# A two-layer diffusion trunk on one core: four-tile first pieces, weight and modulation loads a step ahead, single tiles in the whole half-steps

## The chip, the cores and the metric

One program on one core of a Trainium2 chip. The metric is device time in microseconds; three runs of the kernel before are given, and one more execution that the hardware profiler recorded. The engines are TensorE (PE, matmuls; PEld its weight loads), VectorE (DVE), ScalarE (ACT), GpSimd (POOL) and SyncE (SP, which issues most transfers).

## The reference, cut to what matters

512 latent tokens and 256 context tokens of width 1024 go through two layers. All numbers are fp32.

```python
for l in range(2):
    mx = split(silu(c) @ w_mod[l] + b_mod[l], 9)       # latent: shift, scale, gate, three times
    my = split(silu(c_ctx) @ w_mod[l] + b_mod[l], 9)   # context
    x = x + 0.5 * mx[2] * swiglu(modulate(rmsnorm(x), mx[0], mx[1]), w1[l,0], w3[l,0], w2[l,0])
    # y (context) alike with my
    ox, oy = mixer(modulate(rmsnorm(x), mx[3], mx[4]), ...)   # pooling | retention | convolution
    x = x + mx[5] * ox
    x = x + 0.5 * mx[8] * swiglu(modulate(rmsnorm(x), mx[6], mx[7]), w1[l,1], w3[l,1], w2[l,1])
    # y alike, except behind the last layer's mixer input, where it is no longer needed
return rmsnorm(x) * final_g
# swiglu(h) = (silu(h @ w1) * (h @ w3)) @ w2, with 2816 = 22 x 128 hidden columns
# modulate(h, shift, scale) = h * (1 + scale) + shift
```

## The kernel before

Activations lie with features on the 128 partitions and tokens along the columns; latent is a group of 512 columns, context one of 256. Every product of high precision is three matmuls (`mm3`, lines 162 to 167): operands are split into a high part that ScalarE rounds (line 159) and a low part that VectorE gets by subtraction (line 160), and high x high, high x low and low x high are added in PSUM.

**Weights.** `weight_order` (519) lists all weight blocks in the order of use. `fetch` (566) asks SP for a block into one of five `raw` buffers, `parts` (575) splits it into one of four `wh` and `wl` buffers, and `blocks` (582) does one after the other; `weights` (624) keeps up to four split blocks ahead. An item that is a list (two blocks, `w1` and `w3` of a halved tile) is fetched as soon as the item before it is split; a plain item is fetched only when its own turn to be split comes.

**Feed-forward.** Four times: layer 0 first (`ffn`, 662), layer 0 second and layer 1 first (`ffn_halved`, 801), layer 1 second (`ffn` again, latent only). The 22 hidden tiles are taken in pieces, `PIECES = (2, 4, 4, 4, 4, 4)`. In `ffn` a piece is first `up` (641: products with w1 and w3, silu, product, split into `g`) tile by tile and group by group, then `down` for the eight output tiles, which VectorE adds to x with the gate (693). In the first `ffn` the first two tiles of `up` are in `begun` (1355), among the start of the program. Behind the first piece line 685 drains the task `self.first`, the gate of this feed-forward, before any `down`.

`ffn_halved` works in half-steps of two hidden tiles. The first two half-steps (tiles 0 to 3, "whole") use `up` as above, with both tiles of the half-step in one call per group, so that a call holds four PSUM banks. Meanwhile `differences` (720) makes sums and differences of the activations on VectorE for the other tiles, which `up_halved` (745) computes by seven products of half the columns and depth instead of eight. `down` takes two output tiles of both groups at a time, four PSUM banks; ScalarE evicts each with its gate to `xpart` (229) and GpSimd adds it to x kept in DRAM (231). The last four tiles are one step, whose `down` adds on VectorE (842) and sums squares for the next norm (419).

**Modulation.** The gate, shift and scale vectors come from `w_mod` blocks of 512 KB. `mod_chunks` (364) goes through them: a step asks SP for a block into one of two `wm` buffers (373), VectorE multiplies it by the conditioning and accumulates (319, 321; four instructions per block), behind four blocks it folds (329, 330), and behind eight a small matmul `mods` (337) sums over partitions.

**What sets the order.** The program is straight-line, written out by Python, with semaphores put in by the framework; each engine runs its own queue in order. Side work is a generator that `spawn` enters with a due time. A planner's clock advances by `spent`, 0.001266 us per column of each `mm3`; `poll`, behind each step of the products, runs what is due, and `drain` runs tasks until those named are done, whatever the time. `mod_chunks` yields its pace per block and 11.71 us before `mods`. The framework may put an engine's instructions in another order than they are written when a buffer or an operand is not yet there by its own estimate.

Of the kernel before, what the change touches and what calls it, by code (L numbers as in the profile page):

```python
# [20 lines left out]
DEPTH = 2  # L21
DFF = 2816
NF = DFF // P
PIECES = (2, 4, 4, 4, 4, 4)
MAXP = max(PIECES)
HEADS = 4
WINDOWS = (2, 4, 8, 16)
# [54 lines left out]
class Kernel:  # L82
# [103 lines left out]
    def setup(self):  # L186
        nc = self.nc
        self.pp = self.const([P, NPP], "pp")
        nc.sync.dma_start(self.pp, self.ins["pp"])
        self.cs = self.const([P, NCS], "cs")  # L190
        nc.sync.dma_start(self.cs, self.ins["cs"])
        self.norms, self.kept = {}, {}
        self.x = {LAT: [None] * KD, CTX: [None] * (KD // 2)}
        self.ahead, self.plan, self.look = [], self.blocks(), 0
        self.ident = self.cs[:, CS_ID : CS_ID + P]
        self.ones = self.const([P, P], "ones")
        nc.vector.memset(self.ones, 1.0)
        self.fold = self.cs[:, CS_FOLD : CS_FOLD + P]

        self.sc = self.const([P, KD, 2], "sc")  # L200
        nc.scalar.activation(
            self.sc, self.pp[:, PP_C : PP_C + 2 * KD].rearrange("p (k v) -> p k v", v=2), AF.Silu
        )
        self.mod, self.gs, self.gates = {}, {}, {}
# [159 lines left out]
    def mod_chunks(self, ljs, pace):  # L364

        nc = self.nc
        for l, j in ljs:
            rows = self.tiny(64, "mrow")
            for half in range(2):
                acc = [self.slot("macc") for _ in range(2)]  # L370
                for kk in range(4):
                    raw = self.wide("wm").rearrange("p (k n) -> p k n", k=2)
                    nc.sync.dma_start(raw, self.ins["w_mod"][l, j, half, kk])
                    for k in range(2):
                        self.mod_add(acc, raw[:, k], kk * 2 + k)
                    yield -pace
                self.mod_fold(acc, rows[:, half * 32 : half * 32 + 32])
            yield 11.71
            self.mod_sums(l, j, (0, 1), rows)
# [139 lines left out]
    def weight_order(self):  # L519
# [3 lines left out]
        def halved(l, s):  # L523
            f0 = 0
            for npc in PIECES:
                w2 = ins["w2"][l, s, :, f0 * D : (f0 + npc) * D].rearrange("p (d f n) -> p d f n", d=KD, f=npc)
# [13 lines left out]
        def ffn(l, s):  # L540
            f0 = 0
            for npc in PIECES:
                for f in range(f0, f0 + npc):
# [38 lines left out]
    def blocks(self):  # L582


        nc = self.nc
        order = self.weight_order()
        src = next(order)
        raws = None
        while src is not None:
            if raws is None:  # L590
                raws = self.fetch(src)
            after = next(order, None)
            early = None
            if not isinstance(src, list):
                if isinstance(after, list):
                    early = self.fetch(after)
                self.parts(raws[0])
                yield
            else:
                w1, w3 = raws  # L600
                half = slice(0, 512), slice(512, 1024)
                b, c = self.raw(1024), self.raw(1024)
                nc.vector.tensor_sub(b[:, half[0]], w1[:, half[0]], w3[:, half[0]])
                nc.vector.tensor_add(c[:, half[0]], w3[:, half[0]], w3[:, half[1]])
                self.parts(w1)
                yield
                nc.vector.tensor_sub(b[:, half[1]], c[:, half[0]], w1[:, half[0]])
                self.parts(b)
                early = self.fetch(after) if after is not None else None
                yield  # L610
                nc.vector.tensor_sub(c[:, half[1]], w1[:, half[1]], b[:, half[1]])
                self.parts(c)
                yield
                self.parts(w3[:, half[1]])
                yield
            src, raws = after, early
# [45 lines left out]
    def ffn(self, l, s, h, starts, grps, ends, done, begun=None):  # L662
# [4 lines left out]
        accs = {}  # L667
        for pi, npc in enumerate(PIECES):
            g = self.empty()
# [131 lines left out]
    def ffn_halved(self, l, s, h, starts, grps, ends, done):  # L801
        nc = self.nc
        idx = 2 * s
        accs = {}
        T = {i: [[None] * HK for _ in range(2)] for i in (2, 3, 4)}
        f0 = 0
        while f0 < NF:
            g = self.empty()
            n = SUB if f0 < NF - PIECES[-1] else PIECES[-1]
            last = f0 + n == NF  # L810
            per = 8 // n

            def load():
                for st in (CTX, LAT):
                    self.load_x(st, self.kept[st])

            if f0 < WHOLE:
                ws = {f: self.w13() for f in range(n)}
                for grp in starts if f0 == 0 else grps:
                    self.need(grp)  # L820
                    if f0 == 0 and grp is starts[-1]:
                        task = self.spawn(self.differences(h, T), 1.0)
                    self.up(ws, range(n), h, g, grp)
                if f0 + n == WHOLE:
                    self.drain(task)
                    self.first_difference(h)
            else:
                for f in range(n):
                    self.up_halved(f, h, T, g, load if last and f == n - 1 else None)
            w2 = []  # L830

            def down(dt, grp, ps, fs):
                self.products([(ps, w2[dt // per], dt % per * n * P + fs[0] * P)], g, grp, fs, fs[0] == 0, fs[-1] == n - 1)

            if last:
                w2 = [self.weights() for _ in range(KD // per)]
                for grp in ends:
                    for dt in range(KD):
                        ps = self.psum("down")[:, : grp[2]]
                        down(dt, grp, ps, range(n))  # L840
                        xd = self.xs(dt, grp)
                        nc.vector.scalar_tensor_tensor(xd, ps, self.gate(l, idx, grp[0], dt), xd, op0=ALU.mult, op1=ALU.add)
                        self.square(dt, grp, accs)
                    done(grp, accs)
            else:
                for d in range(0, KD, 2):
                    if d % per == 0:
                        w2.append(self.weights())
                    these = [(dt, grp, self.psum("down")[:, : grp[2]]) for dt in (d, d + 1) for grp in grps]
                    for fs in ((0,), (1,)):  # L850
                        for dt, grp, ps in these:
                            down(dt, grp, ps, fs)
                    for dt, grp, ps in these:
                        self.add_kept(dt, grp, ps, self.gate(l, idx, grp[0], dt))
            f0 += n
# [447 lines left out]
    def run(self):  # L1303
        nc = self.nc
# [8 lines left out]
        h = self.rows()  # L1313
# [41 lines left out]
        def begun(g):  # L1355
# [6 lines left out]
                self.up({f: w0[f]}, [f], h, g, grp, ps[grp, f])  # L1362
            self.up(w0, [1], h, g, G_CTX)

        self.first = [self.spawn(self.mod_chunks([(0, 2)], 4.0), 10.0)]
        later = self.spawn(self.mod_chunks([(0, j) for j in range(3, 9)], 6.0), 80.0)
        for l in range(DEPTH):
            last = l == DEPTH - 1
            grps = (G_LAT,) if last else both
            cuts = halves if last else both  # L1370

            def next_norm(l, idx):
                tiles = self.rows()
                return tiles, lambda grp, accs: self.norm(l, idx, grp, accs, tiles)

            h1, done = next_norm(l, 1)
            if not last:
                self.ffn(l, 0, h, both, both, both, done, begun)
                self.drain(later)
                self.decays()  # L1380
            else:
                later = self.spawn(self.mod_chunks([(l, j) for j in range(5, 9)], 9.5), 110.0)
                self.ffn_halved(l, 0, h, both, both, both, done)
                self.drain(later)

            h2, done = next_norm(l, 2)
            self.mixer(l, h1, grps, cuts, done)

            if not last:
                later = self.spawn(self.mod_chunks([(l + 1, j) for j in range(5)], 8.0), 110.0)  # L1390
                h, done = next_norm(l + 1, 0)
            else:
                done = self.final
            (self.ffn if last else self.ffn_halved)(l, 1, h2, cuts, grps, cuts, done)
            self.drain(later)
# [134 lines left out]
```

## Time and profile before

| | us |
|---|---|
| median of three runs (2642.98 to 2646.76) | 2646.35 |
| profiled execution | 2645.3 |
| its span, first to last instruction | 2643.5 |
| TensorE busy | 2536.2 (96%) |
| VectorE busy | 1808.0 (68%) |
| ScalarE busy | 1017.6 (38%) |
| GpSimd busy | 276.3 (10%) |
| TensorE's mean granted clock, share of full | 0.983 |

In the span the first feed-forward runs to about 600 us, the mixer of layer 0 to about 925, the halved feed-forwards from there to about 1487 and 2015, the second mixer to about 2260, and the last feed-forward to the end. Matmuls are pipelined: one of 512 columns is recorded with 0.39 us and the next begins 0.23 us behind it. A wait is the idle time of an engine before an instruction, put down to what ended it.

### The profile page before, as it was taken

How to read it: one execution, taken by the hardware profiler on the slowest of the kernel's cores; microseconds unless marked ns; L12 is line 12 of the kernel's file. 1: busy time of each engine (PE TensorE's matmuls, PEld its weight loads, DVE VectorE, ACT ScalarE, POOL GpSimd, SP SyncE). 2: the span in 40 equal slices, each digit the busy share in tenths (PEclk: the TensorE clock that was granted, in tenths of full speed). 3: DMA queues.
4: the chain of work that ended last, by engine and by line, in shares of the span. 5: the costliest groups of instructions: out<-in, count | busy, mean ns of one | idle time of the engine just before them, and what ended most of it. 6: DMA issues, size and time to landing. Idle time of an engine off the chain costs nothing. (4 is left out here: it accounts for less than half of the span.)

```text
span 2643.5 us, 36683 instructions
## 1 busy us (share of the span) xinstructions
PE 2536.2 (96%) x14002; PEld 2250.5 (85%) x14002; DVE 1808.0 (68%) x3390; ACT 1017.6 (38%) x1780; POOL 276.3 (10%) x316
## 2 busy tenths in 40 slices
PE   8699999999999999998999889999999999999998
PEld 4588888888898888998999679999998888888887
DVE  6766866536987674886879656786787686744335
ACT  3121121124235544554554345555544254422223
POOL 0000000000000122232330023233220001000000
PEclk9899999999999999999999899999999999999999
DMA  6443544222321744686686247768664334222231
GB/s 252 129 135 120 160 128 122 87 62 85 111 80 55 201 92 96 167 208 167 159 206 207 74 102 154 183 162 195 170 169 153 104 100 108 92 96 96 96 97 47
DMA packets 149265, 345.37 MB, mean 131 GB/s; under 512 B 15712, under 2 KB 54112, under 8 KB 149088
## 3 DMA queue, kind: packets, MB, share of 16 engines
q1 hardware_dynamic: 101088, 276.94, 31.9%
q0 software_dynamic: 44928, 61.89, 14.6%
q10 hardware_dynamic: 3072, 4.20, 0.6%
q8 instruction: 109, 1.79, 0.3%
q14 instruction: 68, 0.56, 0.1%
HBM read 263.27 MB, written 75.50 MB: 128 GB/s over the span
## 5 line engine op out<-in xcount | busy, mean ns | idle before, releaser
L159 ACT CAST wh<-raw 128x1024 fp32r<-128x1024 f32 (+1 forms) x400 | 399.9, 1004 | 894.7 <-PE up L165 362.4
L160 DVE TENSOR_TENSOR wl<-raw,wh 128x1024 fp32r<-128x1024 f32 (+1 forms) x400 | 462.7, 1162 | 357.8 <-ACT wh L159 348.5
L164 PE MATMUL up<-h,wh 128*128 128x512 f32 (+2 forms) x1920 | 659.9, 345 | 9.2 <-ACT half L767 6.7
L165 PE MATMUL up<-h,wh 128*128 128x512 f32 (+2 forms) x1920 | 659.8, 344 | 0.2
L166 PE MATMUL up<-h,wl 128*128 128x512 f32 (+2 forms) x1920 | 658.6, 344 | 0.0
L231 POOL DMA_DIRECT2D xkept<-xpart x312 | 276.1, 1378 | 1957.7 <-ACT xpart L229 1914.3
L164 PE MATMUL down<-g,wh 128*128 128x256 f32 (+1 forms) x1264 | 428.9, 348 | 23.2 <-ACT g L159 16.2
L165 PE MATMUL down<-g,wh 128*128 128x256 f32 (+1 forms) x1264 | 435.4, 346 | 0.4 <-DVE g L160 0.4
L166 PE MATMUL down<-g,wl 128*128 128x256 f32 (+1 forms) x1264 | 431.4, 344 | 0.0
L164 PEld LDWEIGHTS up<-h,wh 128*128 128x128 f32 x1920 | 363.8, 190 | 43.7 <-ACT half L767 8.2
L165 PEld LDWEIGHTS up<-h,wh 128*128 128x128 f32 x1920 | 364.7, 190 | 32.7 <-DVE h L508 0.7
L166 PEld LDWEIGHTS up<-h,wl 128*128 128x128 f32 x1920 | 364.2, 190 | 31.5
L321 DVE SCALAR_TENSOR_TENSOR macc<-wm,sc,macc 128x512 f32<-128x512 f32 x462 | 321.5, 744 | 33.0 <-DMA wm<-in_w_mod_dram 32.8
L164 PEld LDWEIGHTS down<-g,wh 128*128 128x128 f32 x1264 | 239.5, 193 | 55.7 <-ACT g L159 18.7
L165 PEld LDWEIGHTS down<-g,wh 128*128 128x128 f32 x1264 | 242.4, 192 | 29.6 <-DVE g L160 2.4
L166 PEld LDWEIGHTS down<-g,wl 128*128 128x128 f32 x1264 | 242.0, 192 | 29.4
L229 ACT ACTIVATE xpart<-down,gate 128x256 f32<-128x256 f32 (+1 forms) x288 | 154.4, 586 | 68.1 <-PE down L166 62.0
L164 PE MATMUL up<-t,wh 128*128 128x384 f32 x432 | 145.3, 336 | 3.7 <-ACT half L767 3.7
L656 DVE TENSOR_TENSOR silu<-silu,up 128x256 f32<-128x256 f32 (+1 forms) x84 | 48.3, 576 | 146.6 <-PE up L166 139.6
L693 DVE SCALAR_TENSOR_TENSOR x<-down,gate,x 128x512 f32<-128x512 f32 (+1 forms) x152 | 95.5, 635 | 72.8 <-PE down L166 71.8
L166 PE MATMUL up<-t,wl 128*128 128x384 f32 x432 | 144.9, 335 | 0.0
L165 PE MATMUL up<-t,wh 128*128 128x384 f32 x432 | 144.7, 335 | 0.0
(210 smaller groups left out, 3298.9 us busy)
## 6 DMA issues: line engine op xcount, KB each, us to landing
raw<-in_w_dram SPq DMA_DIRECT2D x260, 512.0 KB, 3.9
wm<-in_w_mod_dram SPq DMA_DIRECT2D x128, 512.0 KB, 4.1
xkept<-xpart POOLq DMA_DIRECT2D x160, 256.0 KB, 9.6
xkept<-xpart POOLq DMA_DIRECT2D x152, 128.0 KB, 9.1
raw<-in_w_feat_dram SPq DMA_DIRECT2D x36, 512.0 KB, 3.7
xkept<-x SPq DMA_DIRECT2D x44, 256.0 KB, 3.3
x<-xkept SPq DMA_DIRECT2D x44, 256.0 KB, 6.0
wm<-in_w_mod_dram SPq DMA_DIRECT2D x32, 256.0 KB, 5.4
```

What stands on the lines that cost most here:

```text
L159: self.nc.scalar.copy(hi, src)
L160: self.nc.vector.tensor_sub(lo, src, hi.bitcast(F32))
L164: nc.tensor.matmul(out, wh, xh, start=start, stop=False, skip_group_check=shared)
L165: nc.tensor.matmul(out, wh, xl, start=False, stop=False, skip_group_check=shared)
L166: nc.tensor.matmul(out, wl, xh, start=False, stop=stop, skip_group_check=shared)
L229: self.nc.scalar.activation(part, ps, AF.Copy, scale=gate)
L231: self.nc.gpsimd.dma_start(self.kept[st][:, c0 : c0 + n], part, accum_op=ALU.add)
L321: self.nc.vector.scalar_tensor_tensor(acc[v], raw, s, acc[v], op0=ALU.mult, op1=ALU.add)
L656: nc.vector.tensor_mul(t, t, ps[f, 1])
L693: nc.vector.scalar_tensor_tensor(xd, ps, self.gate(l, idx, grp[0], dt), xd, op0=ALU.mult, op1=ALU.add)
```

## The change

`PIECES` becomes `(4, 4, 4, 4, 2, 4)` (the layout of w2 follows it). `mod_chunks` asks for its first block before it begins and for each next block a pace before the one at hand is accumulated. `blocks` fetches the next item before it splits the present one, for plain items too, from the first feed-forward's main loop on (`self.early`). In the whole half-steps the tiles are taken one by one: in the first, context is still taken with both tiles, latent one tile after the other; in the second, each tile takes context and then latent. `down` of a half-step goes through both output tiles of a group before the next group. Paces and first due times of the modulation tasks of the two halved feed-forwards change.

```diff
-PIECES = (2, 4, 4, 4, 4, 4)
+PIECES = (4, 4, 4, 4, 2, 4)
...
     def mod_chunks(self, ljs, pace):
...
+        steps = [(l, j, half, kk) for l, j in ljs for half in range(2) for kk in range(4)]
+
+        def load():
+            raw = self.wide("wm").rearrange("p (k n) -> p k n", k=2)
+            nc.sync.dma_start(raw, self.ins["w_mod"][steps.pop(0)])
+            return raw
+
+        after = load()
...
                 for kk in range(4):
-                    raw = self.wide("wm").rearrange("p (k n) -> p k n", k=2)
-                    nc.sync.dma_start(raw, self.ins["w_mod"][l, j, half, kk])
+                    raw, after = after, load() if steps else None
+                    yield -pace
                     for k in range(2):
                         self.mod_add(acc, raw[:, k], kk * 2 + k)
-                    yield -pace
...
-                if isinstance(after, list):
+                if after is not None and (self.early or isinstance(after, list)):
                     early = self.fetch(after)
...
-                ws = {f: self.w13() for f in range(n)}
-                for grp in starts if f0 == 0 else grps:
-                    self.need(grp)
-                    if f0 == 0 and grp is starts[-1]:
-                        task = self.spawn(self.differences(h, T), 1.0)
-                    self.up(ws, range(n), h, g, grp)
+                if f0 == 0:
+                    ws = {f: self.w13() for f in range(n)}
+                    for grp in starts[:-1]:
+                        self.up(ws, range(n), h, g, grp)
+                    self.need(starts[-1])
+                    task = self.spawn(self.differences(h, T), 1.0)
+                for f in range(n):
+                    if f0:
+                        ws = {f: self.w13()}
+                    for grp in grps if f0 else starts[-1:]:
+                        self.up(ws, [f], h, g, grp)
...
-                    these = [(dt, grp, self.psum("down")[:, : grp[2]]) for dt in (d, d + 1) for grp in grps]
+                    these = [(dt, grp, self.psum("down")[:, : grp[2]]) for grp in grps for dt in (d, d + 1)]
...
-                later = self.spawn(self.mod_chunks([(l, j) for j in range(5, 9)], 9.5), 110.0)
+                later = self.spawn(self.mod_chunks([(l, j) for j in range(5, 9)], 9.0), 90.0)
...
-                later = self.spawn(self.mod_chunks([(l + 1, j) for j in range(5)], 8.0), 110.0)
+                later = self.spawn(self.mod_chunks([(l + 1, j) for j in range(5)], 7.4), 90.0)
```

## Rows read from the trace of the kernel before

**Rows 1.** The page, busy us (share of the span) and instructions.
```profile
PE 2536.2 (96%) x14002; PEld 2250.5 (85%) x14002; DVE 1808.0 (68%) x3390; ACT 1017.6 (38%) x1780; POOL 276.3 (10%) x316
```
**Rows 2.** Timeline of TensorE: start, us, instruction, form, count, idle before and releaser.
```profile
101.06 0.47 PE L337 MATMUL mods<-mrow,cs 128*128 128x64 f32 x1 [23.03 <-DVE mrow L330]
```
**Rows 3.** Waits of TensorE, whole span: us in total, times, longest.
```profile
PE down L164 <- ACT g L159: 16.2, 7, 3.4
PE up L164 <- ACT half L767: 10.3, 6, 6.4
...
PE down L164 <- ACT xpart L229: 7.0, 4, 1.7
```
**Rows 4.** Stretches: us, busy per engine (count), TensorE clock, DMA share, GB/s.
```profile
200.00:600.00 400.00, 400.00 (x2329) 354.59 (x2329) 252.39 (x427) 81.59 (x117) 0.00 (x0) 1.00 0.36 112
...
83.16:107.05 23.89, 5.99 (x21) 5.42 (x22) 19.35 (x40) 0.00 (x0) 0.00 (x0) 0.50 0.46 145
...
sum 17.07, PE 15.50 PEld 12.94 DVE 14.30 ACT 4.81 POOL 0.00; mean PE 3.88 PEld 3.24 DVE 3.58 ACT 1.20 POOL 0.00
...
1240.28:1247.10 6.82, 4.73 (x15) 4.73 (x16) 6.75 (x11) 3.15 (x6) 0.00 (x0) 0.50 0.66 195
...
sum 13.65, PE 9.33 PEld 7.22 DVE 8.88 ACT 2.37 POOL 0.00; mean PE 4.66 PEld 3.61 DVE 4.44 ACT 1.18 POOL 0.00
...
2008.28:2011.69 3.41, 3.41 (x10) 2.75 (x10) 2.05 (x15) 0.00 (x0) 0.00 (x0) 0.50 0.00 0
```
**Rows 5.** Waits of TensorE at 950:1040, 1440:1490 (two rows), 2000:2015, 2280:2295.
```profile
PE down L164 <- ACT g L159: 6.2, 2, 3.4
...
PE ms L427 <- DVE acc L419: 9.6, 2, 6.4
PE rstd L443 <- DVE diag L434: 5.1, 2, 3.1
...
PE ms L427 <- DVE acc L419: 2.4, 1, 2.4
...
PE down L164 <- ACT g L159: 2.2, 1, 2.2
```
**Rows 6.** Groups of VectorE, 66.1 to 101.1 us: count, busy us, mean ns, idle before.
```profile
L321 DVE SCALAR_TENSOR_TENSOR macc<-wm,sc,macc 128x512 f32<-128x512 f32 x28 | 19.1, 745 | 1.3 <-DMA wm<-in_w_mod_dram 1.3
L160 DVE TENSOR_TENSOR wl<-raw,wh 128x512 fp32r<-128x512 f32 x4 | 2.7, 686 | 1.3 <-PE up L165 1.3
...
L160 DVE TENSOR_TENSOR g<-silu,g 128x256 fp32r<-128x256 f32 (+1 forms) x4 | 2.2, 551 | 0.1
L656 DVE TENSOR_TENSOR silu<-silu,up 128x256 f32<-128x256 f32 (+1 forms) x4 | 2.2, 544 | 0.0
```
**Rows 7.** Timeline of VectorE, then ScalarE, in the first whole half-step.
```profile
954.78 3.50 DVE L160 TENSOR_TENSOR wl<-raw,wh 128x1024 fp32r<-128x1024 f32 x3 [5.73 <-ACT wh L159]
...
968.93 1.04 ACT L159 CAST wh<-raw 128x1024 fp32r<-128x1024 f32 x1 [2.22 <-PE down L165]
...
970.30 3.88 ACT L229 ACTIVATE xpart<-down,gate 128x256 f32<-128x256 f32 x8
```
**Rows 8.** Timeline of VectorE: first and last of a latent norm; a w_mod accumulation.
```profile
931.28 2.06 DVE L504 SCALAR_TENSOR_TENSOR ht<-x,G,rstd 128x512 f32<-128x512 f32 x3 [2.00 <-PE rstd L443]
...
941.53 0.74 DVE L510 SCALAR_TENSOR_TENSOR h<-ht,mod,h 128x512 fp32r<-128x512 f32 x1
...
1238.26 0.75 DVE L321 SCALAR_TENSOR_TENSOR macc<-wm,sc,macc 128x512 f32<-128x512 f32 x1 [5.93 <-DMA wm<-in_w_mod_dram]
```
**Rows 9.** Groups of VectorE, 1440 to 1482 us.
```profile
L321 DVE SCALAR_TENSOR_TENSOR macc<-wm,sc,macc 128x512 f32<-128x512 f32 x12 | 8.8, 745 | 0.0
```
**Rows 10.** Waits of ScalarE, VectorE and SP, whole span.
```profile
ACT wh L159 <- DMA raw<-in_w_dram: 6.8, 5, 5.6
...
DVE raw L603 <- DMA raw<-in_w_dram: 45.5, 14, 5.9
...
SPq L373 <- DVE macc L321: 456.4, 112, 14.4
```

More of the change, by code (lines that the diff above doesn't have):

```diff
@@ L193, in setup @@
         self.x = {LAT: [None] * KD, CTX: [None] * (KD // 2)}
-        self.ahead, self.plan, self.look = [], self.blocks(), 0
+        self.ahead, self.plan, self.look, self.early = [], self.blocks(), 0, False
         self.ident = self.cs[:, CS_ID : CS_ID + P]
@@ L1363, in begun @@
             self.up(w0, [1], h, g, G_CTX)
+        self.early = True
         self.first = [self.spawn(self.mod_chunks([(0, 2)], 4.0), 10.0)]
```

## The prediction

> **What bounds the kernel now.** I read the page's busy shares first: TensorE is busy for 2536.2 us, 96% of the span [rows 1]. No matmul is added or removed, so the change can only win TensorE's idle time and the time in which its clock is low. The next view is therefore what TensorE waited for: 23.0 us once, for the gate sums (`mods`, line 337) [rows 2]; 16.2 us in 7 waits of `down` for the split of `g`, 10.3 us of the halved products for the copied `half` (one wait of 6.4 is most of it), 7.0 us in 4 waits of `down` for a PSUM buffer that ScalarE had not evicted [rows 3]. The third view, stretches, gives the clock. The long stretch of full work runs at clock 1.00, at 400 / 2329 = 0.172 us per matmul where as many have 256 as 512 columns (split one to two: 0.115 and 0.23). Stretches at 0.50 (1.2 of 2.4 GHz) begin inside or just behind idle time of TensorE, and each loses half of its busy time: 5.99 / 2 = 3.0 us behind the `mods` wait, 15.50 / 2 = 7.75 over the four stretches in the two layers' whole half-steps (at 960, 1018, 1527 and 1582), 4.73 / 2 = 2.4 at 1240, 9.33 / 2 = 4.7 over the two at 1459 and 1479, 3.41 / 2 = 1.7 at 2008 [rows 4]. Last, the waits by place [rows 5].
>
> **The change part by part.** Everything is counted against the profiled execution, 2645.3 us (2643.5 of span and 1.8 around it), 1.05 under the median of the three runs.
>
> *First piece of four tiles, layer 0.* TensorE stops for 23.0 us because the first `down` stands behind `mods`, which needs 32 accumulations on VectorE. With four tiles it has two more tiles of `up` first: 2 x 96 matmuls x 0.172 = 33.0 us, from 78.0 (the wait's start, 101.06 - 23.03) to 111.0. Does VectorE finish by then? From 66 to 101 it was nearly full: 19.1 us of accumulation, 2.7 of weight splits (four of 512 columns), 2.2 of silu products and 2.2 of g splits among the rest [rows 6]. New beside it: four splits become 1024 wide, 3.50 / 3 = 1.17 each [rows 7], so 4 x (1.17 - 0.69) = 1.9; up to four more, 4.7; three quarters of another 4.4 of silu and g, 3.3. Together 9.9. Less 1.3 + 1.3 of its waits [rows 6] that earlier loads and a fuller queue spare, `mods` is ready at 101.1 + 9.9 - 2.6 = 108.4, before 111.0. I take 23.0 + 3.0 less 1.0 for a tight finish: **25.0**. Bounds: 26 if nothing remains, 14 if VectorE is 12 us later than this.
>
> *The same edit elsewhere.* The last feed-forward loses its 2.2 us wait behind a two-tile first piece [rows 5]; a two-tile piece now stands fifth in both plain feed-forwards. There the last tile's silu is early, but its product, split and low part (about 0.6 each, [rows 6]) have 0.7 to 1.4 us of matmuls before they are missed: about 0.75 lost each time. **+0.7**, bounds -3 and +2. Shorter or longer runs of the w2 loads only change places between half-steps: 0.
>
> *Whole half-steps one by one, `down` by groups.* Today both tiles of a pair end together; four weight buffers come free at once, and VectorE does three weight splits (3.50 us) before the silu product that `down` waits for [rows 7]: 6.2 us in layer 0 and 6.2 in layer 1, alike [rows 5]. One by one, three of the four buffers come free 5 us or more earlier, and `down` has 12 context and 6 latent matmuls, 12 x 0.115 + 6 x 0.23 = 2.8 us, before it needs the last latent g, against 0.6 + 0.6 and one cast of 1.05 = 2.3. I take the waits as gone, 12.4, with their clock, 7.75: **20.2**. Bounds 0 (VectorE's queue stays as it is) and 20.2. In the later half-steps the first tile's four products come first in either order: 0.
> The four waits for a PSUM buffer, 7.0 us, have another cause: ScalarE stood in a cast that waits for `down` itself (968.93), and eight evictions came behind it at 970.30 [rows 7]. The earlier casts may or may not undo that order: half, **3.5**, bounds 0 and 7.
> What is late next is the latent norm. VectorE makes eight normalised tiles in 942.27 - 931.28 = 11.0 us [rows 8], the first after about 2.7; a pair used one per 12 x 0.23 = 2.8 us, the first matrix of a single tile uses all eight in 24 x 0.23 = 5.5. Taken strictly in order TensorE waits up to 11.0 - 2.7 - 5.5 = 2.8 us at each of two places; if the second matrix's products are put between, nothing. I take **-2**, bounds -6 and 0.
>
> *w_mod blocks a step ahead.* VectorE's in-order queue sits in an accumulation for 5.93 us until its block lands [rows 8], and 6.4 us of TensorE [rows 3] with 2.4 of clock hang on it. Now the block is asked for one pace earlier, with two buffers held in turn. Gain 6.4 + 2.4 less 1: **7.8**, bounds 0 and 8.8. Queued behind the new request on SP are weight blocks (rival 2).
>
> *Paces and delays.* In layer 0's second feed-forward the chunks are due 110 + 5 x (8 x 8.0 + 11.71) = 488.6 after their start on the planner's clock, whose `spent` adds up to 62.2 (whole up) + 245.0 (halved up) + 171.1 (down) = 478, with the last `down` from 447. So twelve accumulations (8.8 us [rows 9]) stand in VectorE's queue among the squares, and the drain puts the latent norm ahead of the next step's context products, so nothing fills its waits. New: 90 + 5 x (8 x 7.4 + 11.71) = 444.6, before the last `down`. Waits of 9.6 + 5.1 [rows 5] and 4.7 of clock go; I leave 4.1 as at 2007 (2.4 + 1.7), the same place of the next layer: **15.3**, bounds 8 and 19. At 2007 itself the end moves from 460.8 to 424.8, out of the tail: **3.0** of 4.1, bounds 0 and 4.1. The denser pace adds small waits in the halved steps: **-2**, bounds -8 and 0.
>
> *Weight blocks an item ahead.* ScalarE waited for a weight block 6.8 us in all, 5 times [rows 10]; five raw buffers already let SP run ahead. **0**, bounds -2 and +2.
>
> Sum: 25.0 + 0.7 + 20.2 + 3.5 - 2 + 7.8 + 15.3 + 3.0 - 2 = 71.5. 2645.3 - 71.5 = 2573.8, with the 1.05 to the median **2575 us**.
>
> **The rivals.**
> 1. *The whole half-steps' waits stay* (20.2 + 3.5 not won): 2599. For it: VectorE has `differences` in its queue there as well, so the last g can still be late. Against: the three splits of [rows 7] alone are longer than the wait they cause, and they spread out. The Trainium skill has a rule that leans this way, in "Perfetto Trace Analysis", Optimization Strategy: the same gap coming back on the engine that should be full can mean too few SBUF or PSUM buffers. By it the waits for a PSUM buffer would all stay, since no buffer is added; the trace agrees that a buffer is waited for, and shows ScalarE's queue holding it back.
> 2. *Slower: w_mod requests hold SP.* SP waited 456.4 us for `macc` to free a w_mod buffer [rows 10]. A request now stands a pace earlier in SP's order, and the weight blocks behind it wait with it. In the halved steps those land just in time: VectorE waited 45.5 us for them, 14 times [rows 10]. The halved feed-forwards have 72 requests. If each held a weight block for one block's accumulation, 4 x 0.68 = 2.7 us [rows 6], and TensorE paid half of it, that is 97 us: 2575 + 97 = 2672. It decides from (71.5 + 5.3) / 72 = 1.1 us of TensorE's time per request. Against: the weight blocks' own buffers also come free only when VectorE gets to them, and TensorE has paid little of the 45.5. The Trainium skill bears on the place: "DMA: Bandwidth & Descriptors", Anatomy of one DMA, has it that a DMA engine never waits on a semaphore, the issuing sequencer does, before it dispatches. The trace agrees, with SP's 456.4 us.
> 3. *The chunks still end late* (the planner counts no stalls): 15.3 + 3.0 not won, 2593. For it: 444.6 is only 2 us before the last `down`. Against: it is 44 us earlier than before, and 36 at 2007.
> 4. *An edit does nothing*: weight blocks an item ahead. That is in the forecast already.
>
> **How the numbers follow.** Forecast 0.68, with its own range 2562 to 2588 (13 us either way: the PSUM waits, the latent norm and the pace at their bounds); rival 1 0.13; rival 3 0.10; rivals 1 and 3 partly together 0.05; rival 2 at a size that decides 0.04. Rivals 1 and 3 add 24 and 18, and the forecast may do 19 better at the best of every bound, so the range is 2556 to 2608. A difference under 0.2%, 5.3 us, can't be told from none here. Any one of the three large terms makes it faster: 0.95; within 0.2% 0.02 and slower 0.03, both from rival 2 and a little of the mixed case.
>
> **What would show it.** `mods` waits 3 us or less and no clock of 0.50 stands near 100 us; the waits of `down` for g fall from 16.2 to under 4; the wait of 6.4 for `half` is gone, and VectorE waits for w_mod only a few us; no accumulation stands behind the last halved `down` of layer 0, and `ms` and `rstd` there wait under 5 us; TensorE's matmuls are as many as before. I am wrong if `mods` still waits over 10 us, if the halved products show new waits of over 1 us per w_mod block, or if VectorE's waits for weight blocks grow well past 45.5.

## The result and the profile after

The changed kernel takes 2601.44 us (median of four runs, 2599.37 to 2605.04) against 2646.56 of the kernel before (2642.98 to 2649.17) measured beside it: ratio 0.9832, 95% interval 0.9815 to 0.9849. It is 45 us faster; the forecast was 71.5. The range of 2556 to 2608 holds it; the forecast's own range of 2562 to 2588 does not. The profiled execution took 2599.37 us with a span of 2597.6, 45.9 us less than the span before.

First the changed kernel's busy shares, to be read against [rows 1]: TensorE executes the same 14002 matmuls in a shorter span.

```profile
PE 2526.9 (97%) x14002; PEld 2241.7 (86%) x14002; DVE 1813.5 (70%) x3390; ACT 1014.6 (39%) x1780; POOL 277.4 (11%) x316
```

Then what TensorE waits for in it, whole span (us in total, times, longest). The lines answer to [rows 2, 3 and 5].

```profile
PE up L164 <- ACT half L774: 25.6, 14, 3.8
...
PE ms L434 <- DVE acc L426: 7.1, 4, 3.6
PE down L164 <- ACT g L159: 4.3, 3, 2.1
PE down L164 <- ACT xpart L229: 3.5, 2, 1.8
PE up L164 <- ACT xpart L229: 3.5, 2, 1.7
PE rstd L450 <- DVE diag L441: 3.4, 2, 2.7
```

Most of what the prediction wanted gone is gone: there is no line for `mods`, the waits for g fall from 16.2 to 4.3 (the prediction's sign was under 4), those of `ms` from 17.5 to 7.1. But the halved products' wait for `half` has grown from 10.3 in 6 times to 25.6 in 14. All waits in the two stretches of halved half-steps together are 31.1 us, against 12.0 before. The next view, stretches, shows the same (us, busy per engine, TensorE's clock, DMA share, GB/s). In the kernel before, some 9 and 3 us of TensorE were missing in the halved half-steps of layer 0 and layer 1:

```profile
1037.00:1437.00 400.00, 391.10 (x2242) 374.24 (x2241) 311.56 (x511) 207.05 (x361) 105.76 (x120) 0.99 0.74 184
...
1600.00:1995.00 395.00, 392.37 (x2252) 375.38 (x2251) 294.12 (x477) 209.22 (x365) 108.68 (x124) 1.00 0.75 183
```

The changed kernel has full work where `mods` had stopped TensorE (first line), but some 14 and 17 us are missing in the halved half-steps. Little is missing in the tail that had lost most [rows 5]. Four short places in the halved half-steps have clock 0.50.

```profile
60.00:101.00 41.00, 41.00 (x251) 36.78 (x250) 36.84 (x58) 15.37 (x24) 0.00 (x0) 1.00 0.44 143
...
1002.00:1411.00 409.00, 394.98 (x2242) 375.98 (x2241) 324.58 (x537) 205.12 (x359) 105.04 (x119) 0.99 0.74 186
1411.00:1440.00 29.00, 27.43 (x144) 23.16 (x143) 24.75 (x59) 14.45 (x27) 0.00 (x0) 1.00 0.43 158
1545.00:1957.00 412.00, 395.17 (x2251) 374.60 (x2251) 298.31 (x491) 207.64 (x364) 110.18 (x124) 1.00 0.72 176
...
1212.35:1215.76 3.41, 3.41 (x12) 3.41 (x12) 3.41 (x6) 0.14 (x1) 0.00 (x0) 0.50 0.41 136
1260.13:1263.55 3.42, 3.42 (x13) 3.42 (x12) 3.42 (x6) 0.72 (x2) 0.00 (x0) 0.50 0.53 177
1365.94:1369.36 3.42, 3.42 (x13) 3.42 (x12) 2.96 (x5) 1.43 (x2) 0.00 (x0) 0.50 0.68 212
1758.48:1761.89 3.41, 3.41 (x12) 3.41 (x13) 3.41 (x6) 0.73 (x1) 0.00 (x0) 0.50 0.43 154
```

Here is one of the new waits in the changed kernel's timelines (start, us, instruction, count, idle before and releaser), VectorE first:

```profile
1593.66 1.03 DVE L319 TENSOR_SCALAR macc<-wm,sc 128x512 f32<-128x512 f32 x2
1594.61 4.05 DVE L321 SCALAR_TENSOR_TENSOR macc<-wm,sc,macc 128x512 f32<-128x512 f32 x6
1598.58 0.68 DVE L160 TENSOR_TENSOR wl<-raw,wh 128x512 fp32r<-128x512 f32 x1
1604.11 5.61 DVE L321 SCALAR_TENSOR_TENSOR macc<-wm,sc,macc 128x512 f32<-128x512 f32 x8 [4.85 <-DMA wm<-in_w_mod_dram]
1609.64 1.22 DVE L160 TENSOR_TENSOR wl<-raw,wh 128x1024 fp32r<-128x1024 f32 x1
1610.77 0.55 DVE L788 TENSOR_TENSOR half<-up,half 128x384 f32<-128x384 f32 x1
```

then SP's queue, where the first count of 2 covers two requests:

```profile
1596.04 2.98 SPq L371 DMA_DIRECT2D wm<-in_w_mod_dram  x2
```

and ScalarE, then TensorE:

```profile
1611.36 0.52 ACT L789 ACTIVATE half<-half 128x384 f32<-128x384 f32 x1 [4.27 <-DVE half L788]
1611.79 0.46 ACT L774 COPY half<-up 128x384 f32<-128x384 f32 x1
...
1612.30 0.44 PE L164 MATMUL up<-h,wh 128*128 128x384 f32 x1 [1.97 <-ACT half L774]
```

The accumulations of four blocks stand in a run in VectorE's queue (four instructions per block). The first two blocks have landed: VectorE goes through them without a stop. The third can be asked for only when the first is used up (1596.04) and lands 8 us later, so VectorE idles 4.85 us in the middle of the run. Behind the run stand a weight split and the sum at L788. ScalarE waits 4.27 us for that sum (L789), its copy at L774 stands behind, and TensorE waits 1.97 us for the copy.

The theory that follows is **T**: the new paces and due times put the accumulations where such a run meets work that TensorE needs, and VectorE stands before blocks that two buffers let come no earlier. It has these rivals: the block asked for a pace ahead does the harm by itself; or single tiles, `down` by groups or the earlier weight fetch do; or the accumulations' own work, landed or not, is in the way.

### The profile page after: what moved, and what is told of

Same layout as the page of the kernel before. It is cut to its first block, busy times and chain, and to the rows that moved or that the text cites. A ratio compares the mean times of both kernels' runs of the same rounds, so it can differ in the third digit from the quotient of the medians.

```text
span 2597.6 us, 36705 instructions
## 1 busy us (share of the span) xinstructions
PE 2526.9 (97%) x14002; PEld 2241.7 (86%) x14002; DVE 1813.5 (70%) x3390; ACT 1014.6 (39%) x1780; POOL 277.4 (11%) x316
## 3 DMA queue, kind: packets, MB, share of 16 engines
q1 hardware_dynamic: 101088, 276.94, 31.1%
q0 software_dynamic: 44928, 61.89, 15.4%
## 5 line engine op out<-in xcount | busy, mean ns | idle before, releaser
L164 PE MATMUL down<-g,wh 128*128 128x256 f32 (+1 forms) x1264 | 425.0, 344 | 7.9 <-ACT g L159 4.3
L165 PE MATMUL down<-g,wh 128*128 128x256 f32 (+1 forms) x1264 | 430.1, 342 | 0.9 <-DVE g L160 0.9
L321 DVE SCALAR_TENSOR_TENSOR macc<-wm,sc,macc 128x512 f32<-128x512 f32 x462 | 320.9, 745 | 59.9 <-DMA wm<-in_w_mod_dram 59.3
L164 PEld LDWEIGHTS down<-g,wh 128*128 128x128 f32 x1264 | 236.0, 189 | 41.1 <-ACT g L159 9.1
L165 PEld LDWEIGHTS down<-g,wh 128*128 128x128 f32 x1264 | 239.3, 189 | 29.7 <-DVE g L160 3.5
```

What stands on the lines that cost most here:

```text
L164: nc.tensor.matmul(out, wh, xh, start=start, stop=False, skip_group_check=shared)
L165: nc.tensor.matmul(out, wh, xl, start=False, stop=False, skip_group_check=shared)
L321: self.nc.vector.scalar_tensor_tensor(acc[v], raw, s, acc[v], op0=ALU.mult, op1=ALU.add)
```

## The experiments

Each kernel is the changed one with the edit shown, save `only_pieces`. Kernels of one group ran on one chip and share the runs of the kernel before; ratios are to those. Two columns are read from the profiles: TensorE's waits for `half`, and VectorE's waits for a w_mod block (`macc`), whole span, us.

| kernel | median us | ratio, 95% interval | `half` | w_mod |
|---|---|---|---|---|
| before | 2646.56 | 1 | 10.3 | 32.8 |
| changed | 2601.44 | 0.9832, 0.9815 to 0.9849 | 25.6 | 59.3 |
| undo_mod | 2620.53 | 0.9902, 0.9885 to 0.9918 | 37.9 | 65.5 |
| undo_pace | 2597.56 | 0.9808, 0.9790 to 0.9826 | 8.9 | 33.6 |
| undo_mod_pace | 2599.71 | 0.9821, 0.9806 to 0.9836 | 12.1 | 27.4 |
| undo_two | 2604.33 | 0.9842, 0.9825 to 0.9859 | 27.5 | 59.4 |
| start60 | 2561.22 | 0.9681, 0.9666 to 0.9695 | 4.3 | 28.7 |
| wm3 | 2578.47 | 0.9740, 0.9725 to 0.9754 | 5.8 | 5.7 |
| delay75 | 2575.92 | 0.9735, 0.9720 to 0.9749 | 12.9 | 43.5 |
| undo_whole | 2618.25 | 0.9890, 0.9874 to 0.9907 | 26.7 | 61.4 |
| noahead | 2602.25 | 0.9829, 0.9811 to 0.9847 | 23.8 | 57.2 |
| start60_wm3 | 2562.30 | 0.9682, 0.9663 to 0.9701 | 3.8 | 4.0 |
| delay60 | 2587.42 | 0.9773, 0.9755 to 0.9791 | 19.7 | 36.4 |
| only_pieces | 2617.06 | 0.9886, 0.9867 to 0.9904 | 10.6 | 28.4 |

### Which edit makes the new waits (first group)

`undo_mod` (the list of steps and the function `load` go too):
```diff
...
-                    raw, after = after, load() if steps else None
-                    yield -pace
+                    raw = self.wide("wm").rearrange("p (k n) -> p k n", k=2)
+                    nc.sync.dma_start(raw, self.ins["w_mod"][l, j, half, kk])
...
+                    yield -pace
```


> The changed kernel with mod_chunks as it was before (a step asks for its block and accumulates it at once). TensorE's waits in the two halved feed-forwards are 31.1 us in the changed kernel against 12.0 before, and four stretches of clock 0.50 (some 6.8 us) are new there. If the load a step ahead is the cause (it puts the accumulations at other places of VectorE's queue), the waits fall to 12-16 us and the time to 2575-2582. If the denser pace is the cause, the waits stay at 25-33 us and the time at 2596-2606. If a load a step ahead is a gain after all, as forecast (7.8), the waits grow to 36-40 us and the time to 2607-2612.

It is slower still, beyond the third case: 2620.53 us, with 37.9 us of waits for `half`. With these paces the new `mod_chunks` is a gain of 19 us, so it does not do the harm by itself.

`undo_pace`:
```diff
-                later = self.spawn(self.mod_chunks([(l, j) for j in range(5, 9)], 9.0), 90.0)
+                later = self.spawn(self.mod_chunks([(l, j) for j in range(5, 9)], 9.5), 110.0)
...
-                later = self.spawn(self.mod_chunks([(l + 1, j) for j in range(5)], 7.4), 90.0)
+                later = self.spawn(self.mod_chunks([(l + 1, j) for j in range(5)], 8.0), 110.0)
```


> The changed kernel with the old paces and first due times (9.5 and 8.0, 110). In every case the accumulations of layer 0 end late again: 14-20 us of ms and rstd waits at 1400-1425 with some 4 us of clock, and 3-4 us in the next layer's tail. If the denser pace makes the new waits of the halved half-steps, these fall to 12-16 us from 31.1 and the time is 2594-2604, the two cancelling. If the load a step ahead makes them, they stay at 28-34 us and the time is 2618-2628.

It takes 2597.56 us, as the first case has it. Its waits are shown first in the tail of layer 0 (1396 to 1465), then over the whole span:

```profile
PE ms L434 <- DVE acc L426: 7.8, 2, 5.1
PE rstd L450 <- DVE diag L441: 7.3, 2, 4.2
...
PE up L164 <- ACT half L774: 8.9, 5, 5.1
```

The tail waits 15.1 us again, and the halved half-steps wait 5.1 us in each layer. The new paces and due times give at one place what they take at the other: the two kernels' intervals overlap. (The expectation of `undo_mod` calls the four stretches of clock 0.50 new. The kernel before had two such places in the halved half-steps, at 1240 [rows 4] and 1950: 2.4 + 1.7 us lost, against 4 x 3.41 / 2 = 6.8.)

`undo_mod_pace`: both edits above.

> The changed kernel with mod_chunks, paces and first due times all as before. If these two edits together make the new waits (the accumulations stand in another order on VectorE), the halved half-steps wait 12-16 us as before, the tails wait again (18-24 us), and the time is 2594-2604. If the other edits make them (single tiles, down by groups, the earlier fetch of weight blocks), the halved half-steps still wait 28 us or more and the time is 2618-2628.

It takes 2599.71 us, with 12.1 us of waits for `half`, as in the first case. With the old paces the new `mod_chunks` makes no difference that can be told (2597.56 with it).

`undo_two`:
```diff
-        self.early = True
...
-                    these = [(dt, grp, self.psum("down")[:, : grp[2]]) for grp in grps for dt in (d, d + 1)]
+                    these = [(dt, grp, self.psum("down")[:, : grp[2]]) for dt in (d, d + 1) for grp in grps]
```


> The changed kernel with weight blocks fetched as before (a plain item in its own turn) and down in its old order (both groups of an output tile, then the next). If w_mod's accumulations are the cause of the new waits, these stay at 27-35 us and the time at 2596-2607. If down by groups or the earlier fetch makes them, they fall to 12-18 us and the time to 2577-2588.

It takes 2604.33 us, with waits as in the changed kernel. These two edits are not the cause, and together they are worth nothing that can be told; neither was tried by itself.

### Spacing, place or landing (second group)

`start60`: old paces, earlier start.
```diff
-                later = self.spawn(self.mod_chunks([(l, j) for j in range(5, 9)], 9.0), 90.0)
+                later = self.spawn(self.mod_chunks([(l, j) for j in range(5, 9)], 9.5), 60.0)
...
-                later = self.spawn(self.mod_chunks([(l + 1, j) for j in range(5)], 7.4), 90.0)
+                later = self.spawn(self.mod_chunks([(l + 1, j) for j in range(5)], 8.0), 60.0)
```


> The changed kernel with the old paces (9.5 and 8.0) and a first due time of 60 instead of 90: the blocks keep their old spacing and still end early on the planner's clock (60 + 378.5 = 438.5, before the last down at 447). If the spacing makes the new waits of the halved half-steps, these are 8-14 us as with the old paces (9.2 there, 31.1 in the changed kernel), the tails don't wait either (under 3 us), and the time is 2572-2584. If it is the place in the half-step at which the blocks fall (the phase), or that a stall moves on to the whole half-steps, the time is 2590-2604.

It takes 2561.22 us, better than either case and 1.5% under the changed kernel by the ratios. Over the whole span `rstd` waits 3.4 us, all of it behind 2100, and there are 4.3 us for `half` and 0.5 for g; the two stretches of halved half-steps lose 4.1 and 0.7 us:

```profile
PE up L164 <- ACT half L774: 4.3, 3, 2.1
...
PE rstd L450 <- DVE diag L441: 3.4, 2, 2.7
...
PE down L164 <- ACT g L159: 0.5, 1, 0.5
```
```profile
1002.00:1398.00 396.00, 391.88 (x2243) 375.27 (x2243) 310.88 (x517) 207.48 (x362) 104.85 (x119) 0.99 0.76 188
1530.00:1922.00 392.00, 391.30 (x2256) 374.28 (x2256) 289.01 (x475) 209.34 (x365) 108.75 (x124) 1.00 0.74 180
```

VectorE still waits 28.7 us for w_mod, but at places that cost little. Its timeline at one:

```profile
1616.95 2.73 DVE L321 SCALAR_TENSOR_TENSOR macc<-wm,sc,macc 128x512 f32<-128x512 f32 x4
1619.61 1.21 DVE L160 TENSOR_TENSOR wl<-raw,wh 128x1024 fp32r<-128x1024 f32 x1
1622.56 2.74 DVE L321 SCALAR_TENSOR_TENSOR macc<-wm,sc,macc 128x512 f32<-128x512 f32 x4 [1.74 <-DMA wm<-in_w_mod_dram]
...
1635.21 0.56 DVE L788 TENSOR_TENSOR half<-up,half 128x384 f32<-128x384 f32 x1 [2.36 <-ACT half L774]
```

The run is through 10 us before L788, and there VectorE waits for ScalarE's copy of a product, not TensorE for VectorE. This edit moves spacing and start together, against the changed kernel; against `undo_pace`, which has the same spacing, only the start moves.

`wm3`:
```diff
-        self.spool = ctx.enter_context(tc.tile_pool(name="slots", bufs=45))
+        self.spool = ctx.enter_context(tc.tile_pool(name="slots", bufs=43))
...
-        return self.wpool.tile([P, 1024], F32, tag="wm", name=self.name(s), bufs=2)
+        return self.wpool.tile([P, 1024], F32, tag="wm", name=self.name(s), bufs=3)
```


> The changed kernel with three w_mod buffers instead of two (and 43 slots instead of 45, to make room). A block is then asked for one accumulation earlier on the device, whatever the written order. If the new waits come from VectorE standing before a block that has not landed (6 to 12 us after a buffer came free), VectorE's waits for w_mod fall from 59 us to under 25, TensorE's waits in the halved half-steps from 31.1 to 10-18 us, and the time is 2577-2590. If it is the accumulations' own work at the wrong place of VectorE's queue, TensorE's waits stay at 25-32 us and the time at 2596-2606.

It takes 2578.47 us at the changed kernel's own paces and due times. The group of accumulations, in the changed kernel and then with three buffers (count, busy us, mean ns, idle before):

```profile
L321 DVE SCALAR_TENSOR_TENSOR macc<-wm,sc,macc 128x512 f32<-128x512 f32 x462 | 320.9, 745 | 59.9 <-DMA wm<-in_w_mod_dram 59.3
```
```profile
L321 DVE SCALAR_TENSOR_TENSOR macc<-wm,sc,macc 128x512 f32<-128x512 f32 x462 | 319.5, 745 | 5.7 <-DMA wm<-in_w_mod_dram 5.7
```

The work is the same, but VectorE hardly stands any more: its waits fall by 53.6 us, and TensorE's waits in the halved half-steps from 31.1 to 11.2 (8.7 and 2.5), less than the 12.0 before. So the new waits came, as far as their sum tells, from blocks that had not landed. What makes the 11.2 that is left, the accumulations' own work or weight blocks, is not shown.

`delay75`:
```diff
-                later = self.spawn(self.mod_chunks([(l, j) for j in range(5, 9)], 9.0), 90.0)
+                later = self.spawn(self.mod_chunks([(l, j) for j in range(5, 9)], 9.0), 75.0)
...
-                later = self.spawn(self.mod_chunks([(l + 1, j) for j in range(5)], 7.4), 90.0)
+                later = self.spawn(self.mod_chunks([(l + 1, j) for j in range(5)], 7.4), 75.0)
```


> The changed kernel with its own paces (9.0 and 7.4) and a first due time of 75 instead of 90: the same spacing, 15 us earlier in the half-steps. If the spacing decides, the halved half-steps wait 26-34 us again and the time is 2596-2606. If the phase decides, the waits move by more than 8 us (below 23 or above 39) and the time with them (under 2594 or over 2610).

It takes 2575.92 us, with 12.9 us of waits for `half`. At the same spacing, the place of the accumulations in the half-steps moves the time by 25 us. With first due times 15 us earlier on the planner's clock the change takes the time that was forecast for it, but not by the forecast's sum: the waits for a PSUM buffer, for one, are all still there.

`undo_whole`:
```diff
-                if f0 == 0:
-                    ws = {f: self.w13() for f in range(n)}
...
-                    for grp in grps if f0 else starts[-1:]:
-                        self.up(ws, [f], h, g, grp)
+                ws = {f: self.w13() for f in range(n)}
+                for grp in starts if f0 == 0 else grps:
...
+                    self.up(ws, range(n), h, g, grp)
```


> The changed kernel with both tiles of a whole half-step in one call per group again. If taking the tiles one by one removed the waits of down for g there (12.4 us, with 7.75 of clock), they come back and the time is 2614-2624. If down by groups or the earlier fetch removed them, the time stays at 2597-2606.

It takes 2618.25 us, by the ratios (0.9890 less 0.9832) 15 us more. Its whole-span waits:

```profile
PE down L164 <- ACT g L159: 14.2, 8, 2.7
...
PE down L164 <- ACT xpart L229: 8.6, 6, 1.8
```

TensorE waits 9.9 us more for g than in the changed kernel (14.2 less 4.3) and 1.6 more for xpart (8.6 against 3.5 + 3.5). Single tiles removed the waits for g; `down` by groups and the earlier fetch, still there, did not.

### The request ahead, and the parts by themselves (third group)

`noahead`:
```diff
...
-        after = load()
...
-                    raw, after = after, load() if steps else None
                     yield -pace
+                    raw = load()
```


> The changed kernel with each w_mod block asked for right before its accumulation is written, not a pace earlier; the planner's times, and with them VectorE's order, stay those of the changed kernel. If two buffers bind the request (in the changed kernel each block is asked for 0.03 us behind the end of the accumulation two blocks before), the earlier request does nothing: 2597-2606, and VectorE's waits for w_mod stay at 55-63 us. If the request ahead is a gain as forecast, 2609 or more, and the waits grow past 70 us.

It takes 2602.25 us. VectorE's 3390 instructions come in the same order in both traces, so only the request differs, and the time does not change. Shown are this kernel's accumulations, then SP's waits for them, here and in the changed kernel:

```profile
L321 DVE SCALAR_TENSOR_TENSOR macc<-wm,sc,macc 128x512 f32<-128x512 f32 x462 | 321.3, 748 | 57.3 <-DMA wm<-in_w_mod_dram 57.2
```
```profile
SPq L371 <- DVE macc L321: 391.2, 117, 15.0
```
```profile
SPq L371 <- DVE macc L321: 390.0, 117, 14.9
```

In either program SP stands at the request and waits for a buffer, 117 times for 128 blocks. What the new `mod_chunks` does to the time (`undo_mod`) it does by moving the accumulations behind the `yield`, a pace later.

`start60_wm3`: `start60` and `wm3` together.

> Old paces, first due time 60, and three w_mod buffers with 43 slots. If landings are what is left of the halved half-steps' waits (4.1 us, VectorE's waits for w_mod 28.7), VectorE's fall under 8 us, TensorE's to about 0-3, and the time is 2554-2563. If the accumulations' own work makes what is left, or two slots fewer cost something now, 2561-2570.

It takes 2562.30 us, which does not tell the two cases apart (their bounds meet there). VectorE's waits fall to 4.0, TensorE's for `half` only from 4.3 to 3.8. With this start, landings cost nothing that can be told.

`delay60`: as `delay75`, with 60.0.

> The changed kernel's own paces (9.0 and 7.4) with a first due time of 60: the spacing of the changed kernel, begun where the 2561 us kernel begins. If the place in the half-step decides and not the spacing, the halved half-steps may wait anything between 4 and 31 us; a time of 2560-2580 says that the dense paces are not bad in themselves, 2590-2606 that they are mostly bad and 75 was a lucky place.

It takes 2587.42 us, between the two cases. Layer 0's halved half-steps, with the pace of 7.4, wait 18.9 us, and layer 1's, with the pace of 9.0, wait 2.6. By layer, VectorE's waits for w_mod and TensorE's waits, us:

| kernel | layer 0, second | layer 1, first |
|---|---|---|
| before | 17.1, 9.4 | 9.7, 2.6 |
| changed | 22.6, 14.3 | 33.0, 16.8 |
| undo_pace | 15.0, 5.1 | 14.1, 5.1 |
| delay75 | 21.4, 8.1 | 18.3, 5.1 |
| delay60 | 29.1, 18.9 | 0.9, 2.6 |
| start60 | 15.7, 4.1 | 6.7, 0.7 |

The rows changed, delay75 and delay60 have one pace per layer and the starts 90, 75 and 60. At one pace TensorE's waits go 14.3, 8.1, 18.9 in layer 0 and 16.8, 5.1, 2.6 in layer 1: the start alone moves them, and not one way only. That the pace has no part in it is not shown: in layer 0 the old pace of 8.0 waits less (5.1 and 4.1) at both of its starts than 7.4 at any of three.

`only_pieces`: the kernel before with
```diff
-PIECES = (2, 4, 4, 4, 4, 4)
+PIECES = (4, 4, 4, 4, 2, 4)
```


> The kernel before with PIECES = (4, 4, 4, 4, 2, 4) alone. If the first piece of four tiles covers the wait for the gate sums by itself (23.0 us, its clock 3.0, and 2.2 of the last feed-forward), the wait before mods is under 2 us and the time 2617-2624. If it needs the earlier w_mod requests too (mods late by 4 to 10 us), 2624-2632.

It takes 2617.06 us, 1.14% or 30 us less than the kernel before (25 to 35 by the interval). Its first gate sums have no idle time ahead of them, where [rows 2] has 23.03:

```profile
111.50 0.33 PE L337 MATMUL mods<-mrow,cs 128*128 128x64 f32 x2
```

## Why the prediction was right, and where it failed

The terms of the sum, as forecast and as the two traces and the experiments show them, us:

| term | forecast | seen |
|---|---|---|
| first piece of four tiles | 25.0 | 26.0: wait 23.0 and clock 3.0 gone |
| the same edit elsewhere | 0.7 | 2.0: 2.21 becomes 0.22 |
| whole half-steps one by one | 20.2 | 18.4: 12.4 + 7.75, less one slow stretch of 3.41 / 2 that stays |
| PSUM waits | 3.5 | 0 |
| latent norm | -2 | 0 |
| chunks out of layer 0's tail | 15.3 | 18.2: 9.6 + 5.1 - 1.2, and 4.7 of clock |
| the same at 2007 | 3.0 | 4.1 |
| w_mod a step ahead, denser pace | 7.8 - 2 | -21.8: waits 12.0 to 31.1, clock 4.1 to 6.8 |
| weight blocks ahead | 0 | 0, tried only together with `down` by groups |

The right column adds up to 46.9, against 45.9 between the spans. So the whole miss sits in one row, and the rest came out within 3.5 us of each term.

That the time still lies in the range is luck. The upper end of 2608 was put there for rivals 1 and 3, and neither came as written; rival 1 had 2599, near the 2601.44, but its waits for g are gone. The row that failed missed by 27.6 us, where its own bounds were -8 and +8.8. (Nor does 2608 follow from the sum beside it: 2575 + 24 + 18 is 2617.)

**The first piece.** Working and cause held. In the changed kernel VectorE's last step before the gate sums ends at 109.91, the first `mods` stands at 110.39, and TensorE is not idle ahead of it:

```profile
109.22 0.69 DVE L330 TENSOR_REDUCE mrow<-mturn 128x16 f32<-128x512 f32 x1
...
110.39 0.33 PE L337 MATMUL mods<-mrow,cs 128*128 128x64 f32 x2
```

The prediction had 108.4 for VectorE and 111.0 for TensorE, so the margin was smaller than forecast, 0.5 us instead of 2.6. The 1.0 left for a tight finish was not needed, and `only_pieces` shows that the piece does it alone.

**Whole half-steps.** Shown by `undo_whole`: single tiles take away the waits for g. The four PSUM waits, of which I took half, all stay, 7.0 us; two only moved, from `down` to the next half-step's `up`. ScalarE still has a cast ahead of its evictions; whether that or the number of buffers holds them was not tried. The rule of the Trainium skill that stood beside rival 1 ("Perfetto Trace Analysis", Optimization Strategy: too few buffers can be behind a gap that comes back) had these waits staying, and they did. It is borne out by a run at another place, w_mod's two buffers (`wm3`).

**Chunks out of the tail.** This was right, and rival 3 did not come. In the changed kernel the whole tail of layer 0 has one wait of over 1 us:

```profile
1422.42 0.71 PE L434 MATMUL ms<-ones,acc 128*128 128x128 f32 x4 [1.18 <-DVE acc L426]
```

**The step that failed** is "Now the block is asked for one pace earlier, with two buffers held in turn. Gain 6.4 + 2.4 less 1", together with the "-2, bounds -8 and 0" of the denser pace. The words "two buffers held in turn" held the objection: in the kernel before, SP already waited 456.4 us for `macc` [rows 10], so the request was bound by the buffer and not by its place in SP's order. `noahead` shows the gain to be nothing. The pace I priced as a matter of spacing alone, and place counts for more than I gave the whole term: at the same pace a due time 15 us earlier takes 25 us off (`delay75`), one 30 us earlier some 15 (`delay60`). The old paces begun at 60 take 40 off (`start60`), and some 34 by the start alone (against `undo_pace`, by the ratios). Of the price, landings are the larger part (`wm3`: 31.1 to 11.2). The place of each run of accumulations in VectorE's queue could not be had from [rows 9 and 10]; the bounds should have been the whole of VectorE's 32.8 us for w_mod, in either direction. The prediction's sign that VectorE waits for w_mod "only a few us" failed with 59.3; its sign for being wrong, over 1 us per block, was set too high to show it (25.6 us over 72 blocks).

Rival 2 did not come: VectorE's waits for weight blocks went from 45.5 [rows 10] to 40.9, so SP held them up no longer than before.

Why a run of four forms where it does is my reading and was not tried by itself. In `down` of a halved half-step VectorE has little but weight splits to do, so accumulations that the planner spreads over `down` are executed in a row, and the third block of a row is the first that two buffers can't have ready.

## What to carry to other kernels

A request written earlier gains nothing while SP already waits for the buffer: look at what the issuing queue waits for before pricing a prefetch. Side work with a period of its own, put into an in-order queue, costs by where in the step it falls (25 us here for a start 15 us earlier), so try two or three start times before judging an edit that moves it. When a forecast's parts are all seen and the sum is not, compare the waits stage by stage; here one stage had lost 21.8 us of the 68.7 that the others had won.

## What was not expected of the hardware

Landing times of w_mod blocks (512 KB), min, median and max us from issue, in the changed kernel at 200 to 420, then at 1545 to 1940 where GpSimd's accumulating transfers run:

```profile
DMA to landing us min/median/max: 3.3/3.5/4.5
...
DMA to landing us min/median/max: 3.4/7.5/12.0
```

The median more than doubles. The changed kernel's queues (packets, MB, share of 16 engines) suggest why; no run takes GpSimd's transfers away to show it:

```profile
q1 hardware_dynamic: 101088, 276.94, 31.1%
q0 software_dynamic: 44928, 61.89, 15.4%
```

GpSimd's queue takes 15.4 / 61.89 = 0.249% per MB, SP's 31.1 / 276.94 = 0.112%: a byte added in DRAM costs 2.2 times the engine time of a byte in SP's transfers. Packet size does not explain it: packets of 2048 bytes took 191 ns in GpSimd's queue and 93 ns in SP's, in the mean over the span. The Trainium skill ("DMA: Bandwidth & Descriptors", Issuing engines are not separate DMA queues) has it that transfers of all issuing engines run on the same 16 and interleave; this trace fits that, with 3.5 us where GpSimd moves nothing and 7.5 where it does.
